# Rows 0 and 1 of the first feed-forward: 544 tokens at once in eight accumulators instead of 256 in four

## The chip, the cores and the metric

The kernel runs on one core of one Trainium2 chip. The core has TensorE (matrix products, PE in the profile; its weight loads are PEld), VectorE (DVE), ScalarE (ACT), GpSimd (POOL) and SyncE (SP, which here only issues loads and stores). Each engine takes its instructions in the order of its own queue and waits on the others by semaphores. Matmul results go to eight accumulators of 128 partitions x 512 float32 values, called banks here.

The metric is the time of one execution on the device in microseconds (us), as the median of several runs. A profile is one further execution, recorded by the hardware; its span runs from its first to its last instruction.

## The reference

One layer of a decoder trunk is computed for 512 prompt tokens and 8 x 4 sample tokens, 544 tokens in all, with 1024 features:

```python
def swiglu(x, wg, wu, wd):
    return (jax.nn.silu(x @ wg) * (x @ wu)) @ wd

x = layer_norm(ALPHA * x + 0.5 * swiglu(x, p["ffn1_wg"], p["ffn1_wu"], p["ffn1_wd"]), p["ln1_g"], p["ln1_b"])
...
x = layer_norm(ALPHA * x + mix, p["ln2_g"], p["ln2_b"])
x = layer_norm(ALPHA * x + 0.5 * swiglu(x, p["ffn2_wg"], p["ffn2_wu"], p["ffn2_wd"]), p["ln3_g"], p["ln3_b"])
```

`mix` comes from a time mixing (RWKV-7) and a short convolution side by side. `wg` and `wu` are 1024 x 2816 and `wd` is 2816 x 1024. The change lies in the first `swiglu`, at the very start of the program: in the first two of the 22 blocks of 128 hidden features, called rows here.

## The kernel before, in words

Tokens lie along the free dimension, features on the 128 partitions. x is kept transposed: eight blocks k of 128 features, each 128 x 544. The tokens are cut into two halves, `HALF = ((0, 256), (256, 544))`, of 256 and 288 tokens.

Every product is made of three matmuls. A number is split into a high part (ScalarE copies it to the rounded type, L134 and L138) and a low part (VectorE subtracts the high part, L135 and L139). The product is high x high, high x low and low x high. So a weight or an x block can be used by TensorE only when ScalarE has made its high part, and for two of the three matmuls VectorE must have followed.

A row m needs its gate (`g`) and its up (`u`) product: for each, eight blocks k of three matmuls, for each half of the tokens. ScalarE then takes the SiLU of the gate product out of its bank, and VectorE multiplies it by the up product.

The program starts as follows. GpSimd fills some constants; ScalarE loads the SiLU table at a first tiny activation (`warm`, L713) and makes the matrix `ones` (L716); four matmuls on constants run. Then SyncE issues the loads of the weights g0, u0, g1, u1 (called w0 to w3: rows 0 and 1) and of the first 256 tokens of x, in pieces of k: blocks 0 to 1, 2 to 3, then 4 to 7 (L722 to L741), each followed in the program by its split. After these, the other 288 tokens of x are loaded in four pieces (L744 and L745), then the two weights of row 2.

- `first_rows` (L431) multiplies the four weights with the 256 tokens, two k at a time across all four products, into four banks; then two SiLUs and two products.
- `main` (L666) goes on. For rows 0 and 1 it does the other 288 tokens (`up(m, 1)`), for rows 2 and 3 both halves. When a row is complete, `put_h` (L363) makes combinations of its two token halves, as needed by a Strassen-like scheme of later products, and splits them. Between the rows, one step of `inputs` (L449) makes and splits similar combinations of x (`next(tv)`).
- Then come the stages `downs` and `pairs` in turn (the scheme's products), whose weights are loaded and split ahead by a plan in units of TensorE work (`plan`, `feed`, `put`).

Banks come from two rings: `mm` (`big()`, three banks) and `sm` (`sm()`, five). `up` takes its banks from `mm`; `first_rows` had four from `sm`.

The order in each engine's queue is found by a scheduler that lists what is ready first. `tc.issue_after(ins)` puts the instructions of a block that run on the same engine as `ins` behind `ins` in its queue, without waiting for its end.

Of the kernel before, what the change touches and what calls it, by code (L numbers as in the profile page):

```python
# [12 lines left out]
F32 = mybir.dt.float32  # L13
F32R = mybir.dt.float32r
AF = mybir.ActivationFunctionType
OP = mybir.AluOpType
# [3 lines left out]
P = 128  # L20
D = 1024
KD = D // P
# [5 lines left out]
T = TP + NSEQ * TS  # L28
B11, B21, B22, NT1, NT2, T3, T4 = range(7)
HALF = ((0, 256), (256, 544))  # L30
# [31 lines left out]
def body(ctx: ExitStack, tc: tile.TileContext, xT, gu1, wd1, win, wo_c, wo_0, wo_1, gu2, wd2, lora, vec, cst,  # L62
         sst, cstate, s0, y_o, wkvp_o, wkvs_o, shift_o, conv_o):
    nc = tc.nc
    PE, ACT, DVE, POOL = nc.tensor, nc.scalar, nc.vector, nc.gpsimd
    dma = nc.sync.dma_start

    def pool(st, name, side="left", **kw):
        return st.enter_context(tc.tile_pool(name=name, bufs=1, side=side, reuse_waits="tile", **kw))
# [9 lines left out]
    xhl = keep.tile([P, 2, KD, T], F32R, name="xhl")  # L79
# [3 lines left out]
    cpb = keep.tile([P, 6 * TB], F32, name="cpb")  # L83
# [9 lines left out]
    def sm():  # L93
        return ps.tile([P, 512], F32, name="sm", bufs=5)
# [15 lines left out]
    def wtiles():  # L110
        return raw_tile(), hl_tile()

    def wload(src, n=1024, parts=1):
        raw, hl = wtiles()
        m = n // parts
        for i in range(parts):
            dma(raw[:, i * m:i * m + m], src[:, i * m:i * m + m])
            wsplit(hl, raw, i * m, i * m + m)
        return hl
# [12 lines left out]

    def wsplit(hl, raw, a, b):
        ACT.activation(hl[:, 0, a:b], raw[:, a:b], AF.Copy)  # L134
        DVE.tensor_tensor(hl[:, 1, a:b], raw[:, a:b], hl[:, 0, a:b].bitcast(F32), op=OP.subtract)  # L135

    def split(hi, lo, x):
        ACT.activation(hi, x, AF.Copy)  # L138
        DVE.tensor_tensor(lo, x, hi.bitcast(F32), op=OP.subtract)  # L139

    def block(hl, j, i):
        if isinstance(hl, tuple):
            hl, i = hl[i // 4], i % 4
        return hl[:, j, i * P:(i + 1) * P]
# [179 lines left out]
    class Ffn:  # L324
# [26 lines left out]
        def weights(self, key, src, n, pair=False):  # L351
            if key not in self.w:
                if pair:
                    raw, hl = raw_tile(), (self.hb_tile(), self.hb_tile())
                    dma(raw[:, 0:n], src)
                    for i in range(2):
                        wsplit(hl[i], raw[:, 512 * i:], 0, min(512, n - 512 * i))
                    self.w[key] = hl
                else:
                    self.w[key] = wload(src, n)  # L360
            return self.w[key]
# [68 lines left out]

        def first_rows(self, o):  # L431

            for a, b in ((0, 2), (2, 4), (4, 6), (6, 8)):
                for i in range(4):
                    hl = self.w["gu"[i % 2], i // 2]
                    for k in range(a, b):
                        for j, (v, y) in enumerate(((0, 0), (0, 1), (1, 0))):
                            PE.matmul(o[i][:, :256], block(hl, v, k), xhl[:, y, k, 0:256], start=(k == 0 and j == 0),
                                      stop=(k == KD - 1 and j == 2), skip_group_check=True)
            for m in range(2):  # L440
                s = self.rows[0][:, m, 0:256]
                ACT.activation(s, o[2 * m][:, :256], AF.Silu)
                DVE.tensor_tensor(s, s, o[2 * m + 1][:, :256], op=OP.mult)
            yield 0

        def first(self):
# [48 lines left out]
        def put(self, key, part):  # L495
# [5 lines left out]
            with ExitStack() as st:  # L501
                for e in self.held:
                    st.enter_context(tc.issue_after(e.ins))
                x = raws[key, "x"]
                if part == "b":
                    hi, lo = (hl[:, j].rearrange("p (q c) -> p q c", q=q) for j in range(2))
                    split(hi, lo, four(x)[:, :, 1])
                elif part == "a":
                    wsplit(hl, raws[key, "a"], 0, 1024)
                else:  # L510
                    if part == "y":
                        a, y = four(raws.pop((key, "a"))), four(raws.pop((key, "x")))
# [153 lines left out]
        def main(self):  # L666
            self.open_tv()
            tv = self.inputs()
            self.raw, self.held, self.t = {}, [], 0
            self.todo, self.events = self.plan()  # L670
            z = self.z
            self.done, self.made = set(), set()
            for i, m in enumerate((3, 0, 1, 2) if self.nf > NEX else range(self.na)):
                if m >= self.nf:
                    yield from self.up(m, 0)
                yield from self.up(m, 1)
                next(tv)
                if i == 1 and self.nf < self.na:
                    for j, n in enumerate("gu"):
                        self.w[n, 3] = wload(self.gu[3, :, j, :])  # L680
                elif i in (1, 2):
                    self.t = (-12, -5)[i - 1]
                    self.feed()
            self.t = 0
            for _ in tv:
                pass
            for d in range(KD):
                ACT.activation(z[:, d], z[:, d], AF.Copy, scale=2.0 * ALPHA)
            for ci in range(LAST + 1):
                if ci:  # L690
                    yield from self.pairs(ci)
                if ci < LAST:
                    yield from self.downs(ci)
            for d in range(KD):
                yield from self.down(LAST, d, 1 - self.late)
# [10 lines left out]
    z = pool(zst, "zp").tile([P, KD, T], F32, name="z")  # L706
# [3 lines left out]
    POOL.memset(one, 1.0)  # L710
    f1 = Ffn(z, gu1, wd1, "1", 2)
    f1.open()
    ACT.activation(warm, one, AF.Silu)  # L713
    POOL.memset(cpb[:, 0:256], 0.0)
    POOL.memset(cpb[:, 256:256 + P], 1.0 / D)
    ACT.activation(onr, cpb[:, 256:256 + P], AF.Copy)  # L716
    firsts = [sm() for _ in range(4)]
    for _ in range(4):
        PE.matmul(firsts[0][:, :256], cpb[:, 0:P], cpb[:, 0:256], start=True, stop=True)
    ws = [wtiles() for _ in range(4)]  # L720

    def first_w(i, a, b):  # L722
        raw, hl = ws[i]
        dma(raw[:, a * P:b * P], gu1[i // 2, :, i % 2, a * P:b * P])
        wsplit(hl, raw, a * P, b * P)

    def first_x(a, b, c0, c1):
        dma(z[:, a:b, c0:c1], xT[:, a:b, c0:c1])
        split(xhl[:, 0, a:b, c0:c1], xhl[:, 1, a:b, c0:c1], z[:, a:b, c0:c1])

    for a, b in ((0, 2), (2, 4), (4, 8)):
        first_w(0, a, b)
        for k in (a, a + 1) if a == 0 else ():
            first_x(k, k + 1, 0, 256)
        if a:
            first_x(a, a + 2, 0, 256)
        first_w(1, a, b)
        if b - a > 2:
            first_x(a + 2, b, 0, 256)
        first_w(2, a, b)  # L740
        first_w(3, a, b)  # L741
    for i, key in enumerate((("g", 0), ("u", 0), ("g", 1), ("u", 1))):
        f1.w[key] = ws[i][1]
    for k in range(0, KD, 2):  # L744
        first_x(k, k + 2, 256, T)  # L745
    for i, n in enumerate("gu"):
        f1.w[n, 2] = wload(gu1[2, :, i, :])
    dma(vc, vec)
# [12 lines left out]
    lo = cpb[:, 0:1024].rearrange("p (a t) -> p a t", a=2)  # L761
# [609 lines left out]
    z = pool(ctx, "zp2", "right").tile([P, KD, T], F32, name="z")  # L1371
# [194 lines left out]
```

## Time and profile before

| What | us |
|---|---|
| median of 3 runs | 1089.46 |
| shortest and longest run | 1087.12, 1090.7 |
| profiled execution | 1087.86 |
| its span | 1086.1 |
| TensorE busy in the span | 1057.3 |
| VectorE, ScalarE, GpSimd busy | 846.2, 588.7, 177.5 |

The granted TensorE clock was 0.998 of full speed. A busy TensorE counts each matmul from its start to its modelled end; matmuls overlap, so its pace is read from the distance of the starts. In the rows of the profile, a line number such as L438 is the line in the kernel; "out<-in" are the tiles written and read; `x96` is a count; "<-" names what ended the idle time before an instruction.

### The profile page before, as it was taken

The page shows a single profiled execution, that of the slowest core. Times are in us where ns is not written, and L with a number is a line of the kernel's source. Part 1 is how long each engine was busy: PE and PEld are TensorE (multiplying, and loading weights), DVE is VectorE, ACT ScalarE, POOL GpSimd, SP SyncE. Part 2 cuts the span into 40 slices and gives each one's busy share as a digit, 9 for nine tenths or more (in the row PEclk, how much of TensorE's full clock was granted, in tenths as well). Part 3 has the DMA queues.
Part 4 walks back from the last instruction along what each step waited for, and adds up shares of the span by engine and source line. Part 5 has one row for each costly group of instructions (what it writes and reads, how often), then busy time and mean ns, then how long its engine had stood idle before and what let it go on. Part 6 is the DMA issues. An engine that isn't in the chain of part 4 may idle for free.

```text
span 1086.1 us, 22868 instructions
## 1 busy us (share of the span) xinstructions
PE 1057.3 (97%) x9258; PEld 1018.5 (94%) x9258; DVE 846.2 (78%) x1576; ACT 588.7 (54%) x1095; POOL 177.5 (16%) x288
## 2 busy tenths in 40 slices
PE   9999999999999999999999999999999999999997
PEld 8999999999999988898889987999999999999996
DVE  7788888889675867775578558999889888888657
ACT  6655565555553677653445334667555565545425
POOL 0122220312200022141001200001312213121000
PEclk9999999999999999999999999999999999999999
DMA  8668595867854233243145625343857859677402
GB/s 280 138 124 191 121 217 132 177 156 148 187 117 154 80 114 84 59 111 85 42 141 185 146 78 178 117 136 78 184 152 153 196 119 211 154 156 177 122 1 83
DMA packets 99081, 148.88 MB, mean 137 GB/s; under 512 B 35232, under 2 KB 60576, under 8 KB 98976
## 3 DMA queue, kind: packets, MB, share of 16 engines
q1 hardware_dynamic: 71776, 111.25, 33.4%
q0 software_dynamic: 27200, 36.18, 22.0%
q8 instruction: 72, 1.18, 0.4%
q14 instruction: 33, 0.27, 0.1%
HBM read 128.74 MB, written 9.75 MB: 128 GB/s over the span
## 4 chain that ended last, share of the span: by engine, by line
PE 67%; issue 10%; DVE 9%; ACT 7%; DMA 6%; SPq 0%; POOL 0%; DVEq 0%; POOLq 0%; ACTq 0%
PE mm L150 7%; PE mm L547 7%; PE mm L151 7%; PE mm L548 7%; PE mm L549 7%; PE mm L152 7%; PE sm L549 5%; PE sm L548 5%; PE sm L547 5%; DMA raw<-in_gu 4%; ACT hl L134 3%; DVE hl L135 2%; PE sm L1047 1%; PE sm L150 1%; PE sm L151 1%
## 5 line engine op out<-in xcount | busy, mean ns | idle before, releaser
L135 DVE TENSOR_TENSOR hl<-raw,hl 128x1024 fp32r<-128x1024 f32 (+3 forms) x232 | 270.6, 1171 | 76.7 <-ACT hl L134 75.6
L134 ACT ACTIVATE hl<-raw 128x1024 fp32r<-128x1024 f32 (+3 forms) x232 | 232.0, 1013 | 90.4 <-DVE raw L514 40.9
L150 PE MATMUL mm<-xhl,hl 128*128 128x288 f32 (+1 forms) x736 | 218.8, 298 | 3.2 <-DVE z L1438 1.6
L151 PE MATMUL mm<-xhl,hl 128*128 128x288 f32 (+1 forms) x736 | 212.9, 289 | 0.3 <-DVE xhl L139 0.3
L152 PE MATMUL mm<-xhl,hl 128*128 128x288 f32 (+1 forms) x736 | 211.5, 288 | 0.1
L150 PEld LDWEIGHTS mm<-xhl,hl 128*128 128x128 f32 x736 | 138.0, 188 | 10.2 <-DVE z L1438 2.6
L151 PEld LDWEIGHTS mm<-xhl,hl 128*128 128x128 f32 x736 | 138.3, 188 | 2.5 <-issue 1.0
L152 PEld LDWEIGHTS mm<-xhl,hl 128*128 128x128 f32 x736 | 138.3, 188 | 1.1 <-DVE hl L135 0.5
L549 PE MATMUL sm<-xhl,hl 128*128 128x272 f32 x432 | 125.3, 290 | 0.0
L548 PE MATMUL sm<-xhl,hl 128*128 128x272 f32 x432 | 124.5, 288 | 0.0
L547 PE MATMUL sm<-xhl,hl 128*128 128x272 f32 x432 | 124.0, 287 | 0.0
L547 PE MATMUL mm<-tv,hl 128*128 128x272 f32 x288 | 83.3, 289 | 3.8 <-ACT cpb L608 2.0
L520 POOL DMA_DIRECT2D raw<-in_gu x36 | 43.4, 1206 | 258.1 <-DVE hlb L139 156.6
L549 PE MATMUL mm<-tv,hl 128*128 128x272 f32 x288 | 83.4, 290 | 0.0
L548 PE MATMUL mm<-tv,hl 128*128 128x272 f32 x288 | 83.1, 289 | 0.0
L547 PEld LDWEIGHTS sm<-xhl,hl 128*128 128x128 f32 x432 | 81.4, 188 | 0.0
L549 PEld LDWEIGHTS sm<-xhl,hl 128*128 128x128 f32 x432 | 81.3, 188 | 0.0
L548 PEld LDWEIGHTS sm<-xhl,hl 128*128 128x128 f32 x432 | 81.2, 188 | 0.0
L526 POOL DMA_DIRECT2D raw<-in_wd x32 | 39.3, 1481 | 249.1 <-DVE hlb L139 218.1
L547 PEld LDWEIGHTS mm<-tv,hl 128*128 128x128 f32 x288 | 54.3, 188 | 5.2 <-ACT cpb L608 3.1
L547 PE MATMUL mm<-hhl,hl 128*128 128x272 f32 x192 | 57.0, 302 | 0.7 <-DVE z L637 0.7
L547 PE MATMUL sm<-hhl,hl 128*128 128x272 f32 x192 | 55.9, 291 | 0.0
(393 smaller groups left out, 2785.5 us busy)
## 6 DMA issues: line engine op xcount, KB each, us to landing
raw<-in_gu SPq DMA_DIRECT2D x84, 512.0 KB, 4.6
raw<-in_gu POOLq DMA_DIRECT2D x36, 512.0 KB, 6.3
raw<-in_wd SPq DMA_DIRECT2D x32, 512.0 KB, 4.7
raw<-in_win SPq DMA_DIRECT2D x26, 512.0 KB, 3.7
raw<-in_wd POOLq DMA_DIRECT2D x32, 256.0 KB, 7.1
raw<-in_wd SPq DMA_DIRECT2D x16, 384.0 KB, 3.2
z<-cpb POOLq DMA_DIRECT2D x16, 272.0 KB, 9.4
z<-sv POOLq DMA_DIRECT2D x16, 272.0 KB, 6.5
```

Source lines behind the costliest of these rows:

```text
L134: ACT.activation(hl[:, 0, a:b], raw[:, a:b], AF.Copy)
L135: DVE.tensor_tensor(hl[:, 1, a:b], raw[:, a:b], hl[:, 0, a:b].bitcast(F32), op=OP.subtract)
L150: PE.matmul(out, wh, src[:, 0, k, c0:c1], start=(start and i == 0), stop=False)
L151: PE.matmul(out, wh, src[:, 1, k, c0:c1], start=False, stop=False)
L152: seen["fill"] = PE.matmul(out, wl, src[:, 0, k, c0:c1], start=False, stop=(stop and i == n - 1))
L520: POOL.dma_start(x.rearrange("p (s c) -> p s c", s=2), bass.AP(tensor=a11.tensor, offset=a11.offset, ap=[[2 * D, P], [P * 2 * D, 2], [1, 5 ...
L526: POOL.dma_start(four(x)[:, i], bass.AP(tensor=a11.tensor, offset=a11.offset, ap=[[DFF, P], [P * DFF, 2], [1, 256]]), accum_op=OP.add)
L547: PE.matmul(out, wh, src(0, i), start=(first and i == 0), stop=False, skip_group_check=True)
L548: PE.matmul(out, wh, src(1, i), start=False, stop=False, skip_group_check=True)
L549: PE.matmul(out, wl, src(0, i), start=False, stop=(i == n - 1), skip_group_check=True)
L1047: crit(PE.matmul(q[r0:r0 + m, o:o + nn], lhs, rhs, start=True, stop=True))
```

## The change

`first_rows` takes all 544 tokens. Each of its four products has two banks, one for each half, so all eight banks are in use: three of `mm` and five of `sm`. The order of the matmuls is by k and then by product for k = 0 to 5; for the last two k it is by product and then by k, so that g0 is done first and u1 last. Rows 0 and 1 need no `up` any more; `main` only calls `put_h` for them.

x is loaded whole, 544 tokens at a time. Its blocks 0 (in two halves) and 1 are loaded from ScalarE's queue, ahead of `warm`; the other six blocks in three loads from SyncE's. SyncE first issues the four weight pieces of k = 0 and 1. The matmuls' number and sizes are the same as before, only their order differs.

The combinations of x (`next(tv)`) are put behind the last weight split (`f1.head`) in VectorE's queue.

```diff
     def wsplit(hl, raw, a, b):
         ACT.activation(hl[:, 0, a:b], raw[:, a:b], AF.Copy)
-        DVE.tensor_tensor(hl[:, 1, a:b], raw[:, a:b], hl[:, 0, a:b].bitcast(F32), op=OP.subtract)
+        return DVE.tensor_tensor(hl[:, 1, a:b], raw[:, a:b], hl[:, 0, a:b].bitcast(F32), op=OP.subtract)
...
         def first_rows(self, o):
-            for a, b in ((0, 2), (2, 4), (4, 6), (6, 8)):
-                for i in range(4):
-                    hl = self.w["gu"[i % 2], i // 2]
-                    for k in range(a, b):
-                        for j, (v, y) in enumerate(((0, 0), (0, 1), (1, 0))):
-                            PE.matmul(o[i][:, :256], block(hl, v, k), xhl[:, y, k, 0:256], start=(k == 0 and j == 0),
-                                      stop=(k == KD - 1 and j == 2), skip_group_check=True)
+            order = [(k, i) for ks in ((0, 1), (2, 3), (4, 5)) for k in ks for i in range(4)]
+            order += [(k, i) for i in range(4) for k in (6, 7)]
+            for k, i in order:
+                hl = self.w["gu"[i % 2], i // 2]
+                for h, (c0, c1) in enumerate(HALF):
+                    for j, (v, y) in enumerate(((0, 0), (0, 1), (1, 0))):
+                        PE.matmul(o[i][h][:, :c1 - c0], block(hl, v, k), xhl[:, y, k, c0:c1], start=(k == 0 and j == 0),
+                                  stop=(k == KD - 1 and j == 2), skip_group_check=True)
             for m in range(2):
-                s = self.rows[0][:, m, 0:256]
-                ACT.activation(s, o[2 * m][:, :256], AF.Silu)
-                DVE.tensor_tensor(s, s, o[2 * m + 1][:, :256], op=OP.mult)
+                for h, (c0, c1) in enumerate(HALF):
+                    ACT.activation(self.rows[0][:, m, c0:c1], o[2 * m][h][:, :c1 - c0], AF.Silu)
+                for h, (c0, c1) in enumerate(HALF):
+                    s = self.rows[0][:, m, c0:c1]
+                    DVE.tensor_tensor(s, s, o[2 * m + 1][h][:, :c1 - c0], op=OP.mult)
             yield 0
...
         def main(self):
...
-                yield from self.up(m, 1)
-                next(tv)
+                if self.nf == 2 and m < 2:
+                    self.done.add(m)
+                    self.made.add(m)
+                    self.put_h(0, m, ("lo", "hi"))
+                    with tc.issue_after(self.head.ins):
+                        next(tv)
+                else:
+                    yield from self.up(m, 1)
+                    with ExitStack() as st:
+                        if self.nf == 2:
+                            st.enter_context(tc.issue_after(self.head.ins))
+                        next(tv)
...
+    def load_x(eng, a, b, c0, c1):
+        eng.dma_start(z[:, a:b, c0:c1], xT[:, a:b, c0:c1])
+
+    def split_x(a, b, c0, c1):
+        split(xhl[:, 0, a:b, c0:c1], xhl[:, 1, a:b, c0:c1], z[:, a:b, c0:c1])
+
+    for h in range(2):
+        load_x(ACT, 0, 1, *HALF[h])
+    load_x(ACT, 1, 2, 0, T)
     ACT.activation(warm, one, AF.Silu)
...
-    firsts = [sm() for _ in range(4)]
+    firsts = [f() for f in (big, big, big, sm, sm, sm, sm, sm)]
+    firsts = [firsts[2 * i:2 * i + 2] for i in range(4)]
...
-    for a, b in ((0, 2), (2, 4), (4, 8)):
-        first_w(0, a, b)
-        for k in (a, a + 1) if a == 0 else ():
-            first_x(k, k + 1, 0, 256)
-        if a:
-            first_x(a, a + 2, 0, 256)
-        first_w(1, a, b)
-        if b - a > 2:
-            first_x(a + 2, b, 0, 256)
-        first_w(2, a, b)
-        first_w(3, a, b)
+    def load_w(i, a, b):
+        dma(ws[i][0][:, a * P:b * P], gu1[i // 2, :, i % 2, a * P:b * P])
+
+    def split_w(i, a, b):
+        return wsplit(ws[i][1], ws[i][0], a * P, b * P)
+
+    for i in range(4):
+        load_w(i, 0, 2)
+        split_w(i, 0, 2)
+        if i == 0:
+            for h in range(2):
+                split_x(0, 1, *HALF[h])
+        elif i == 1:
+            split_x(1, 2, 0, T)
+    for a, b in ((2, 4), (4, 8)):
+        load_x(nc.sync, a, a + 2, 0, T)
+        split_x(a, a + 2, 0, T)
+        for i in range(4):
+            load_w(i, a, b)
+            f1.head = split_w(i, a, b)
+        if b - a > 2:
+            load_x(nc.sync, a + 2, b, 0, T)
+            split_x(a + 2, b, 0, T)
...
-    for k in range(0, KD, 2):
-        first_x(k, k + 2, 256, T)
```

More of the change, by code (lines that the diff above doesn't have):

```diff
@@ L716, in body @@
     ACT.activation(onr, cpb[:, 256:256 + P], AF.Copy)
-    firsts = [sm() for _ in range(4)]
+    firsts = [f() for f in (big, big, big, sm, sm, sm, sm, sm)]
+    firsts = [firsts[2 * i:2 * i + 2] for i in range(4)]
     for _ in range(4):
-        PE.matmul(firsts[0][:, :256], cpb[:, 0:P], cpb[:, 0:256], start=True, stop=True)
+        PE.matmul(firsts[0][0][:, :256], cpb[:, 0:P], cpb[:, 0:256], start=True, stop=True)
     ws = [wtiles() for _ in range(4)]
[L722 to L729, printed above, removed]
-    for a, b in ((0, 2), (2, 4), (4, 8)):
-        first_w(0, a, b)
-        for k in (a, a + 1) if a == 0 else ():
-            first_x(k, k + 1, 0, 256)
-        if a:
-            first_x(a, a + 2, 0, 256)
-        first_w(1, a, b)
+    def load_w(i, a, b):
[16 more added lines that the diff above has]
+            f1.head = split_w(i, a, b)
         if b - a > 2:
-            first_x(a + 2, b, 0, 256)
-        first_w(2, a, b)
-        first_w(3, a, b)
+            load_x(nc.sync, a + 2, b, 0, T)
+            split_x(a + 2, b, 0, T)
     for i, key in enumerate((("g", 0), ("u", 0), ("g", 1), ("u", 1))):
         f1.w[key] = ws[i][1]
-    for k in range(0, KD, 2):
-        first_x(k, k + 2, 256, T)
     for i, n in enumerate("gu"):
```

## The prediction

> **What bounds the kernel now.** I read the totals first. TensorE is busy for 97% of the span and leads the chain that ended last, so a change pays only where TensorE stands still.
>
> ```profile
> PE 1057.3 (97%) x9258; PEld 1018.5 (94%) x9258; DVE 846.2 (78%) x1576; ACT 588.7 (54%) x1095; POOL 177.5 (16%) x288
> ...
> PE 67%; issue 10%; DVE 9%; ACT 7%; DMA 6%; SPq 0%; POOL 0%; DVEq 0%; POOLq 0%; ACTq 0%
> ```
>
> Next, TensorE's timeline around the changed stage (start, length, what).
>
> ```profile
> 4.46 1.84 PE L438 MATMUL sm<-xhl,hl 128*128 128x256 f32 x6
> ...
> 12.93 0.38 PE L438 MATMUL sm<-xhl,hl 128*128 128x256 f32 x1 [0.76 <-ACT xhl L138]
> 13.66 5.79 PE L438 MATMUL sm<-xhl,hl 128*128 128x256 f32 x47 [0.34 <-DVE xhl L139]
> 19.29 0.29 PE L150 MATMUL mm<-xhl,hl 128*128 128x288 f32 x1
> ...
> 31.98 0.28 PE L150 MATMUL mm<-xhl,hl 128*128 128x256 f32 x1
> ```
>
> The 96 matmuls of rows 0 and 1 over 256 tokens (L438) run from 4.46 to 19.29; the 96 over the other 288 tokens follow until row 2 starts at 31.98. The pace is the distance of starts: (19.29 - 13.66) / 47 = 0.120 us for 256 columns, (31.98 - 19.29) / 96 = 0.132 us for 288. At these paces the two parts need 11.5 + 12.7 = 24.2 us, and they took 31.98 - 4.46 = 27.5 us. **The 3.3 us between are all that this stage can give back**; they lie before 13.66, where 49 matmuls (5.9 us) took 9.2 us.
>
> Why TensorE is held there: ScalarE waits for loads, and behind it VectorE and TensorE wait for the split halves.
>
> ```profile
> 0.75 1.28 ACT L713 ACT_TABLE_LOAD   x1 [0.75 <-PEq L1546]
> 2.04 0.20 ACT L713 ACTIVATE warm<-eps 128x1 f32<-128x1 f32 x1
> 2.15 0.29 ACT L716 ACTIVATE ones<-cpb 128x128 fp32r<-128x128 f32 x1
> 3.46 0.42 ACT L134 ACTIVATE hl<-raw 128x256 fp32r<-128x256 f32 x1 [1.02 <-DMA raw<-in_gu]
> 3.79 0.40 ACT L138 ACTIVATE xhl<-z 128x256 fp32r<-128x256 f32 x1
> ...
> 10.50 0.42 ACT L134 ACTIVATE hl<-raw 128x256 fp32r<-128x256 f32 x1 [1.35 <-DMA raw<-in_gu]
> ```
>
> The same start by windows (from:to, length, then busy time and instructions of TensorE, its weight loads, VectorE, ScalarE and GpSimd, clock, share of the DMA engines, GB/s) shows what the loads deliver, and that VectorE has room from row 2 on.
>
> ```profile
> 2.00:5.00 3.00, 3.00 (x9) 2.37 (x8) 0.82 (x3) 1.66 (x7) 0.00 (x0) 1.00 0.83 256
> 5.00:8.00 3.00, 3.00 (x21) 3.00 (x20) 1.98 (x5) 1.60 (x5) 0.00 (x0) 1.00 0.83 245
> 8.00:11.00 3.00, 2.97 (x23) 2.58 (x22) 1.41 (x4) 1.57 (x4) 0.00 (x0) 1.00 0.71 192
> 11.00:14.00 3.00, 1.89 (x14) 1.50 (x13) 2.15 (x4) 2.23 (x4) 0.00 (x0) 1.00 1.06 389
> ...
> 31.90:55.90 24.00, 24.00 (x195) 24.00 (x195) 15.82 (x29) 13.74 (x26) 5.02 (x4) 1.00 0.55 111
> ```
>
> **The change part by part.** Loads are issued by SyncE in order, and each of the first takes 0.40 to 0.45 us of its queue (0.89 / 2):
>
> ```profile
> 0.75 0.40 SPq L724 DMA_DIRECT2D raw<-in_gu  x1
> 1.21 0.89 SPq L728 DMA_DIRECT2D z<-in_xT  x2
> ```
>
> *Matmuls.* None is added or removed: 192 stay, 24.2 us. What changes is how much of each arriving pair of k-blocks feeds TensorE: 24 x 0.120 = 2.9 us before, 24 x (0.120 + 0.132) = 6.05 us after. One (k, row) step is 0.755 us.
>
> *ScalarE's three issues.* No row shows a load issued from ScalarE. Bounds: nothing, or what GpSimd takes, 1206 ns (row below). SyncE's 0.43 us is the nearest row, since like the loads moved it is a plain load without arithmetic; I take it. The three stand ahead of the table load: ScalarE, which finished `ones` 1.69 us after 0.75, is free at 0.75 + 1.29 + 1.69 = 3.73 instead of 2.44. The cover is the 1.02 us that it waited for the first weights, so the first split moves from 3.46 to 3.73. With free issues it stays at 3.46; at GpSimd's price it is 6.06.
>
> ```profile
> L520 POOL DMA_DIRECT2D raw<-in_gu x36 | 43.4, 1206 | 258.1 <-DVE hlb L139 156.6
> ```
>
> The Trainium skill ("DMA: Bandwidth & Descriptors", section "Issuing engines are not separate DMA queues") says that all issuers share the same DMA engines and their transfers interleave, so that a second issuer saves issue time alone. By it the first weights (128 KB) would share the engines with the first 128 KB of x and land up to 0.5 us later (128 KB at the 256 GB/s of 2 to 5 us), at 3.97 instead of 3.46, and the sum below would be worse by 0.2 us. No row before shows two queues at work in this stage.
>
> *The ramp.* Splits, by these rows and by the distance of starts above (0.33 us on ScalarE for 256 columns; x pieces from the 544- to 576-column forms):
>
> ```profile
> L138 ACT ACTIVATE xhl<-z 128x576 fp32r<-128x576 f32 x4 | 2.5, 676 | 0.0
> ...
> L135 DVE TENSOR_TENSOR hl<-raw,hl 128x1024 fp32r<-128x1024 f32 x4 | 4.9, 1218 | 0.0
> L135 DVE TENSOR_TENSOR hl<-raw,hl 128x256 fp32r<-128x256 f32 x8 | 3.2, 423 | 5.7 <-ACT hl L134 5.6
> L139 DVE TENSOR_TENSOR xhl<-z,xhl 128x576 fp32r<-128x576 f32 x4 | 2.9, 753 | 0.3 <-ACT xhl L138 0.3
> ```
>
> ScalarE makes the high halves of w0, x0 (two pieces), w1, x1, w2, w3 from 3.73 to 6.40; VectorE's low halves end at 4.61, 4.95, 5.33, 5.66, 6.49, 6.85 and 7.20. TensorE starts at 4.5, waits about 0.5 us for x0's first low half, 0.1 us for its second and 0.3 us for w2's, and ends k = 0 at 8.15 and k = 1 at 8.15 + 4 x 0.755 = 11.17. Without any wait from 4.46 it would be 10.5.
>
> *Later pairs.* k = 2 and 3 need 2.16 MB (1.05 of weights, 1.11 of x). At the 231 GB/s that 2 to 11 us average, 2.1 MB are in at 11.0, and then 389 GB/s are delivered: complete about 11.3. Add 0.85 us for the two splits of the last quarter: 12.2, against 11.17 + 3 x 0.755 = 13.4 when row u1 first needs it. Block 4 to 8 needs 2.2 MB more, 6 us at 389 GB/s, so 17.3 at the latest for all of it; TensorE reaches k = 4 at 17.2, where only x and w0 are needed. I add 0.2 us for a hiccup here (ends: 0, and 1.5 us if the 192 GB/s of 8 to 11 us lasted on: 2.16 MB after 11.2 us, in at 13.2).
>
> *End of the stage.* 11.17 + 24 x 0.755 + 0.2 = 29.5 for row 2's first matmul, against 31.98: **2.5 us gained.**
>
> *Eight banks.* Row 2 takes the first `mm` bank again. Its gate g0 is done three rows of two k before the end (6 x 0.755 = 4.5 us), at 25.0, and a SiLU of about 0.4 us (next row group) frees it: 25.4 against 29.5. The later two banks are freed by 26.9. Cost nothing, cover 4 us.
>
> *SiLUs, products, `put_h`.* The same instructions, now bunched at 25 to 33 us:
>
> ```profile
> L442 ACT ACTIVATE hk<-sm 128x256 f32<-128x256 f32 x2 | 0.8, 385 | 1.0 <-PE sm L438 1.0
> ...
> L458 DVE TENSOR_TENSOR cpb<-z 128x544 f32<-128x544 f32 x2 | 1.4, 719 | 0.0
> ...
> L443 DVE TENSOR_TENSOR hk<-hk,sm 128x256 f32<-128x256 f32 x2 | 0.8, 414 | 0.0
> ```
>
> VectorE must have the row-2 weights (two splits of 1.22 us) ready by 29.5; what stands before them is 3.4 us (eight weight splits at 0.42), 2.8 us (four of 512 columns, by the line between 0.42 and 1.22 at 0.69) and about 5.5 us of x, with their own 2.4 us 14 us of work from 4 us on: about 11 us of room. The transforms in `inputs` (about 0.72 us each) are only queued behind the last weight split; they are first needed in `pairs`, behind rows 2 and 3 and the first `downs`. The stage from 31.9 to 55.9 moves 2.5 us earlier against a VectorE that is free for 8.2 of 24 us there.
>
> *SyncE.* 15 loads instead of 21 stand before row 2's weights, so these start sooner. GpSimd's queue is not passed. What is late next is TensorE's own work.
>
> The profiled execution took 1087.86 us, 1.8 us more than its span, so the sum is 1085.4. The median shown, 1089.46, is 1.6 us above it; I carry the 2.5 us over and predict 1087.0.
>
> **Rivals.**
> 1. *The start is late or the loads are short:* ScalarE's issues cost GpSimd's price (first split 6.06, 2.3 us lost) or the 1.5 us hiccup happens. Gain 0.2 to 1.2 us, about 1088.7. For it: the 192 GB/s window. Against: SyncE's 0.43 us, and a supply that need only be half as dense per matmul.
> 2. *A queue turns it round (slower):* on VectorE, an in-order engine, the row-2 splits stand behind products and `put_h` of rows 0 and 1, which now wait for the last matmul at 29.5. Two products (0.86 with the larger half), six `put_h` steps of about that size (2.6) and the split (1.22) stop TensorE for 4.7 us: 2.2 us slower, 1091.7; with five transforms of 0.72 between, 5.8 us slower, 1095. It decides once that stall passes 2.5 us. Against: the row-2 weights arrive some 10 us earlier than the products' inputs.
> 3. *Everything goes and something follows:* free issues, no ramp wait, the whole 3.3 us, and a later stage's order improves a little: 1086.0 or lower. Against: TensorE cannot start before x is split.
> 4. *The 2.5 us are given back in the `downs` and `pairs` stages* because weights come late: 1089.5. Against: TensorE's two longest waits in these stages (the waits over the whole span: in total, times, longest) are for ScalarE's copies of its own results; no load and no weight split.
>
> ```profile
> PE mm L547 <- ACT cpb L608: 2.0, 4, 1.0
> ...
> PE mm L547 <- ACT cpb L614: 1.8, 1, 1.8
> ```
>
> **How the numbers follow.** A measurement of this kernel can tell about 0.3%, 3.3 us, from no change. Forecast (1.5 to 3.2 us gained) 0.50; rival 1 0.15; rival 2 0.15; rival 3 0.13; rival 4 0.07. Low end: the shortest run, 1087.12, less 3.3 and 0.8 for a better later order, 1083.0. High end: rival 2's first price and a little, 1092.0. Faster by over 0.3%: rival 3 and a part of the forecast that lies near the bound, 0.23. Slower by over 0.3%: most of rival 2, 0.12. Between them 0.65. By itself the forecast spans 1086.2 to 1088.0.
>
> **What would show it.** The first L438-type matmul at 4.5 to 4.8; no wait of TensorE over 0.5 us after 8 us; row 2's first matmul (128x256) near 29.5; then every stage 2.5 us earlier, the end included. The three issues on ScalarE's queue should take 0.4 us each. I am wrong if row 2 waits for VectorE, if the first split comes after 4.5, or if the shift of row 2 is not the shift of the kernel's end.

## The result and the profile after

Over 20 executions of each kernel on the same chip the changed kernel took 1086.86 us (median; 1082.39 to 1091.17) and the kernel before 1089.95 us (1086.36 to 1094.53). The ratio is 0.9969, with a 95% interval of 0.9955 to 0.9984: faster, by 3.1 us between the medians and by 1.7 to 4.9 us with the interval. The profiled execution took 1082.39 us (span 1080.6), the shortest of its 20, so its end is no fair picture of the median; its start lies among those of the repeats below.

The totals and the chain that ended last, of the changed kernel: TensorE still leads, with 1.2 us less busy time and 5.5 us less span.

```profile
span 1080.6 us, 22860 instructions
...
PE 1056.1 (98%) x9258; PEld 1017.5 (94%) x9258; DVE 845.5 (78%) x1573; ACT 587.1 (54%) x1092; POOL 177.3 (16%) x288
...
PE 75%; DVE 8%; ACT 7%; issue 6%; DMA 4%; POOL 0%; ACTq 0%; DVEq 0%; POOLq 0%
```

TensorE's timeline of the changed stage (start, length, what). The 192 matmuls of rows 0 and 1 are now all on L439, and row 2 begins at 30.48 instead of 31.98.

```profile
4.76 0.58 PE L439 MATMUL mm<-xhl,hl 128*128 128x256 f32 x1
5.59 1.73 PE L439 MATMUL mm<-xhl,hl 128*128 128x288 f32 x8 [0.25 <-ACT xhl L138]
7.16 2.54 PE L439 MATMUL sm<-xhl,hl 128*128 128x288 f32 x15
9.54 1.27 PE L439 MATMUL mm<-xhl,hl 128*128 128x256 f32 x9
...
12.54 1.25 PE L439 MATMUL mm<-xhl,hl 128*128 128x256 f32 x9
...
27.11 3.53 PE L439 MATMUL sm<-xhl,hl 128*128 128x288 f32 x27
30.48 0.28 PE L150 MATMUL mm<-xhl,hl 128*128 128x256 f32 x1
```

The rows split the stage in two. k = 0 (24 matmuls) lasts from 4.76 to 9.54, 4.78 us. From there each k takes 3.00 us (9.54 to 12.54), and the 168 matmuls up to 30.48 take 20.94 us, 0.125 us each, without a wait. The whole loss is in k = 0, which at that pace would have taken 3.0 us.

ScalarE's timeline of the same start: the three loads on its queue, then what it waits for.

```profile
0.74 1.39 ACTq L728 DMA_DIRECT2D z<-in_xT  x3
2.16 1.28 ACT L736 ACT_TABLE_LOAD   x1 [2.16 <-issue]
...
3.99 0.42 ACT L134 ACTIVATE hl<-raw 128x256 fp32r<-128x256 f32 x1
4.31 0.40 ACT L138 ACTIVATE xhl<-z 128x256 fp32r<-128x256 f32 x1
5.10 0.44 ACT L138 ACTIVATE xhl<-z 128x288 fp32r<-128x288 f32 x1 [0.39 <-DMA z<-in_xT]
5.45 0.40 ACT L134 ACTIVATE hl<-raw 128x256 fp32r<-128x256 f32 x1
6.75 0.66 ACT L138 ACTIVATE xhl<-z 128x544 fp32r<-128x544 f32 x1 [0.91 <-DMA z<-in_xT]
7.32 0.71 ACT L134 ACTIVATE hl<-raw 128x256 fp32r<-128x256 f32 x2
```

Block 1 of x (x1) arrives last (6.75), and the splits of w2 and w3, which k = 0 needs, stand behind it in ScalarE's queue (7.32). The same start by windows (columns as in the prediction): 8 to 11 us held 23 matmuls before and holds 24 now, but 11 to 14 us held 14 and holds 26; the DMA engines deliver 332 instead of 192 GB/s in 8 to 11.

```profile
5.00:8.00 3.00, 2.70 (x15) 2.17 (x15) 1.55 (x4) 2.00 (x5) 0.00 (x0) 1.00 1.03 362
8.00:11.00 3.00, 3.00 (x24) 2.88 (x24) 2.22 (x5) 2.37 (x6) 0.00 (x0) 1.00 0.98 332
11.00:14.00 3.00, 3.00 (x26) 3.00 (x25) 2.46 (x5) 2.33 (x4) 0.00 (x0) 1.00 0.97 361
```

The start of the matmuls hides something that the busy column doesn't show. Distances between the starts of the matmuls, in us, listed from the traces:

```
before  4.46 0.57 (5.04), then 0.21 eight times up to 6.75, 0.19, then 0.12 from 6.93 on
after   4.76 0.83 0.41 0.21 0.21 0.21 (6.64) 0.16, then 0.11 to 0.13 from 6.80 on, but for
        0.35 0.22 (ends at 7.77, 7.99) and 0.18 0.22 (ends at 8.56, 8.79)
```

Up to 6.93 and 6.80 us the two kernels run at 0.213 us per 256 columns, about half the later pace, while the granted clock in the windows reads 1.00. That 1.00 is no measurement: the clock's first record in these two traces begins at 6.89 and 6.68, just where the full pace begins, and a window without a record prints 1.00. In the other traces of the kernels that follow, the first record begins anywhere from 5.10 to 7.30 us (without the order: 13.77), so the time at half pace differs from execution to execution.

### The profile page after: what moved, and what is told of

Read it like the earlier page. It is cut to its first block, busy times and chain, and to the rows that moved or that the text cites. A ratio compares the mean times of both kernels' runs of the same rounds, so it can differ in the third digit from the quotient of the medians.

```text
span 1080.6 us, 22860 instructions
## 1 busy us (share of the span) xinstructions
PE 1056.1 (98%) x9258; PEld 1017.5 (94%) x9258; DVE 845.5 (78%) x1573; ACT 587.1 (54%) x1092; POOL 177.3 (16%) x288
## 4 chain that ended last, share of the span: by engine, by line
PE 75%; DVE 8%; ACT 7%; issue 6%; DMA 4%; POOL 0%; ACTq 0%; DVEq 0%; POOLq 0%
PE mm L550 9%; PE mm L551 8%; PE mm L552 8%; PE mm L150 7%; PE mm L151 6%; PE mm L152 6%; PE sm L552 6%; PE sm L550 6%; PE sm L551 6%; DMA raw<-in_gu 3%; ACT hl L134 2%; PE sm L439 1%; PE sm L1072 1%; DVE hl L135 1%; PE sm L150 1%
## 5 line engine op out<-in xcount | busy, mean ns | idle before, releaser
L150 PE MATMUL mm<-xhl,hl 128*128 128x288 f32 (+1 forms) x704 | 209.5, 298 | 3.2 <-DVE z L1463 1.6
L151 PE MATMUL mm<-xhl,hl 128*128 128x288 f32 (+1 forms) x704 | 203.5, 289 | 0.3 <-DVE xhl L139 0.3
L152 PE MATMUL mm<-xhl,hl 128*128 128x288 f32 (+1 forms) x704 | 202.1, 287 | 0.1
L150 PEld LDWEIGHTS mm<-xhl,hl 128*128 128x128 f32 x704 | 132.1, 188 | 10.1 <-DVE z L1463 2.6
L151 PEld LDWEIGHTS mm<-xhl,hl 128*128 128x128 f32 x704 | 132.4, 188 | 2.5 <-issue 1.0
L152 PEld LDWEIGHTS mm<-xhl,hl 128*128 128x128 f32 x704 | 132.3, 188 | 1.1 <-DVE hl L135 0.5
L550 PE MATMUL mm<-hhl,hl 128*128 128x272 f32 x192 | 57.0, 302 | 0.6 <-DVE z L640 0.6
L551 PE MATMUL mm<-hhl,hl 128*128 128x272 f32 x192 | 55.8, 290 | 0.0
```

Source lines behind the costliest of these rows:

```text
L150: PE.matmul(out, wh, src[:, 0, k, c0:c1], start=(start and i == 0), stop=False)
L151: PE.matmul(out, wh, src[:, 1, k, c0:c1], start=False, stop=False)
L152: seen["fill"] = PE.matmul(out, wl, src[:, 0, k, c0:c1], start=False, stop=(stop and i == n - 1))
L550: PE.matmul(out, wh, src(0, i), start=(first and i == 0), stop=False, skip_group_check=True)
L551: PE.matmul(out, wh, src(1, i), start=False, stop=False, skip_group_check=True)
```

## The experiments

The theory: the gain is made at the start of the stage, between the first matmul and row 2, and is only passed on behind it; k = 0 limits it, by data (ScalarE's order and the loads), and perhaps by the half pace. The rivals: the start time of TensorE, ScalarE's load queue, or a stage behind row 2 makes the difference. The table collects all runs; the first three columns come from the traces. "To the end" is from row 2's first matmul to the start of the last matmul. Each ratio is to executions of the kernel before on the same chip.

| Kernel | first matmul of rows 0, 1 | row 2's first | to the end | median us (executions) | ratio to before, 95% |
|---|---|---|---|---|---|
| before | 4.46 | 31.98 | 1046.6 | 1089.95 (20) | |
| before, again | 4.46 | 31.71 | 1045.4 | 1086.42 (1) | |
| after | 4.76 | 30.48 | 1042.5 | 1086.86 (20) | 0.9969 (0.9955 to 0.9984) |
| after, again | 4.80 | 30.94 | 1045.4 | 1090.38 (12) | 0.9992 (0.9974 to 1.0010) |
| x by SyncE | 4.46 | 30.60 | 1046.6 | 1090.75 (12) | 0.9994 (0.9968 to 1.0019) |
| x1 behind w3 | 4.78 | 30.12 | 1051.6 | 1089.53 (12) | 0.9985 (0.9962 to 1.0008) |
| late start | 6.58 | 30.85 | 1050.1 | 1088.24 (12) | 0.9978 (0.9962 to 0.9994) |
| without the order | 5.08 | 34.20 | 1048.2 | 1091.91 (1) | |
| before with x by ScalarE | 4.74 | 31.03 | 1050.3 | 1090.66 (1) | |
| g0 last | 4.79 | 34.98 | 1050.3 | 1094.69 (1) | |
| last chunk held in rows | 4.76 | 30.27 | 1044.5 | 1088.01 (12) | 0.9983 (0.9961 to 1.0005) |
| x1 behind w3, and held in rows | 4.66 | 29.96 | 1050.5 | 1087.93 (12) | 0.9990 (0.9972 to 1.0007) |

**The same two kernels again.** No edit; the point is how much of the first pair's difference comes back.

> The changed kernel once more, unchanged. Theory A (the stage gives 1.5 us for good, and what the profiled executions differ beyond that is the waits of ScalarE for GpSimd's accumulating stores and late weights, which change from one execution to the next): row 2's first matmul again at 30.5 us, within 0.2; the gaps of TensorE ahead of the first product of tv in `pairs` differ from those of the other execution by up to 2 us; median 1.5 to 3.5 us under the kernel before. Theory B (the earlier start moves the later transfers apart for good): those gaps stay at 0.2 to 0.6 us as in the other execution, and the median is 4 us or more under the kernel before.

> The kernel before once more, unchanged, for a second profile. Theory A (from one execution to the next the late waits vary, the start does not): row 2's first matmul at 32.0 us, within 0.3; the time from there to the last matmul, 1046.6 us in the first profile of it, is anywhere from 1042 to 1052, as in the five profiles with the change (1042.5 to 1051.6). Theory B (the change also shortens what follows): it stays above 1046.

Row 2 came at 30.94 in the one, outside the 0.2 us that I allowed, and 31.71 in the other, and the median was 0.6 us under the kernel before instead of 1.5 to 3.5. Before, the two traces have 31.98 and 31.71 (mean 31.85); after, they have 30.48 and 30.94, and a later kernel with the same start 30.27 (mean 30.56). The change of the stage is 1.3 us, of marks that themselves differ by 0.3 and 0.7 us. In the second pair of profiles it is passed on unchanged: 0.8 us at row 2 (31.71 against 30.94) and the same 1045.4 us from there to the end. But the end differs from execution to execution of one kernel: from row 2 on, the changed kernel took 1042.5 and 1045.4 us. One wait that varies this way is ScalarE's for a transfer of `sv` (timelines near 285 us, in this order: before, before again, after, after again):

```profile
286.60 0.43 ACT L572 ACTIVATE sv<-cpb 128x272 f32<-128x272 f32 x1 [3.80 <-DMA z<-sv]
```

```profile
285.20 0.43 ACT L572 ACTIVATE sv<-cpb 128x272 f32<-128x272 f32 x1 [2.23 <-DMA z<-sv]
```

```profile
282.36 0.43 ACT L575 ACTIVATE sv<-cpb 128x272 f32<-128x272 f32 x1 [2.04 <-DMA z<-sv]
```

```profile
284.17 0.43 ACT L575 ACTIVATE sv<-cpb 128x272 f32<-128x272 f32 x1 [2.34 <-DMA z<-sv]
```

The kernel before waited 3.80 us in one execution and 2.23 in the next. TensorE's wait behind such copies goes the same way (waits of before again: in total, times, longest; those of before stand in the prediction):

```profile
PE mm L547 <- ACT cpb L608: 1.2, 3, 0.5
PE mm L547 <- ACT cpb L614: 0.2, 1, 0.2
```

The 1.8 us on which the prediction's rival 4 was judged was 0.2 us in another execution of the same program. So of the 5.65 us by which the first profile of the changed kernel ends its matmuls sooner (1072.95 against 1078.60), 1.5 lie ahead of row 2 and 1.75 between 280 and 300 us, where this wait stands; the other 2.4 arose at several places and were not traced to a wait.

What goes with the column "to the end" is TensorE's clock. In six traces the clock's records show full speed from row 2 to the last matmul (before, before again, after, after again, x by SyncE, last chunk held in rows), and they took 1042.5 to 1046.6 us. The other six have one to three stretches of 3.41 us at half the clock, and took 1048.2 to 1051.6 us. What follows: this change is to be judged at row 2's first matmul.

**x from SyncE's queue, behind w0 and w1.** This undoes the part with ScalarE's queue alone.

```diff
-    for h in range(2):
-        load_x(ACT, 0, 1, *HALF[h])
-    load_x(ACT, 1, 2, 0, T)
...
             for h in range(2):
+                load_x(nc.sync, 0, 1, *HALF[h])
                 split_x(0, 1, *HALF[h])
         elif i == 1:
+            load_x(nc.sync, 1, 2, 0, T)
             split_x(1, 2, 0, T)
```

> Undoes one part: x's blocks 0 and 1 are loaded from SyncE's queue, behind w0 and w1. If a second issuer saves issue time alone and the transfers share the engines (theory A), ScalarE's first split goes back to about 3.5, x1 lands near 6 to 6.5, the other weights some 0.5 us later, and row 2 starts at 30.2 to 30.7, the time within 0.5 us of the changed kernel. If ScalarE's queue brings x in beside the weights at the engines' spare rate (rival), row 2 starts at 31.2 or later.

Row 2 came at 30.60, inside the 30.27 to 30.94 of the change as it is. ScalarE, from this kernel's timeline:

```profile
3.46 0.42 ACT L134 ACTIVATE hl<-raw 128x256 fp32r<-128x256 f32 x1 [1.02 <-DMA raw<-in_gu]
...
8.32 0.42 ACT L134 ACTIVATE hl<-raw 128x256 fp32r<-128x256 f32 x1 [0.94 <-DMA raw<-in_gu]
```

The first weights come at 3.46 again instead of 3.99, and the fourth weight split runs at 8.32 where in the changed kernel it had ended by 8.03 (two from 7.32 in 0.71). What the second queue brings forward at one place it takes at another; in this one trace ScalarE's queue is worth nothing measurable in the changed kernel.

**x by ScalarE's queue in the kernel before.** The reverse: that part alone.

```diff
+    for k in range(2): ACT.dma_start(z[:, k:k + 1, 0:256], xT[:, k:k + 1, 0:256])
     ACT.activation(warm, one, AF.Silu)
...
-        for k in (a, a + 1) if a == 0 else ():
-            first_x(k, k + 1, 0, 256)
+        for k in (a, a + 1) if a == 0 else (): split(xhl[:, 0, k:k + 1, 0:256], xhl[:, 1, k:k + 1, 0:256], z[:, k:k + 1, 0:256])
```

> One part alone, on the kernel before: the 256 tokens of x's blocks 0 and 1 are loaded from ScalarE's queue ahead of its table load, nothing else. With x_sync this makes the square of the two parts. If a second issuer saves issue time alone: ScalarE's first split moves from 3.46 to about 4.0, the later loads come two issues (0.9 us) sooner, and row 2 starts at 31.4 to 32.0, against 31.7 and 32.0 in the two profiles of the kernel before. If ScalarE's queue carries the gain, row 2 starts at 31.0 or earlier.

Row 2 came at 31.03, 0.8 us sooner than the mean before: more than I expected, in one execution. Its windows and ScalarE's timeline say why:

```profile
8.00:11.00 3.00, 3.00 (x28) 3.00 (x27) 1.30 (x4) 1.18 (x4) 0.00 (x0) 1.00 0.92 299
11.00:14.00 3.00, 2.10 (x16) 1.70 (x15) 2.67 (x5) 2.74 (x5) 0.00 (x0) 1.00 1.07 387
```

```profile
3.96 0.42 ACT L134 ACTIVATE hl<-raw 128x256 fp32r<-128x256 f32 x1 [0.59 <-DMA raw<-in_gu]
```

In 8 to 11 us 299 GB/s arrive instead of 192, and 28 matmuls run instead of 23. The first weights come later, at 3.96, and ScalarE waits 0.59 us for them, as it would if the two queues share the engines. So the second queue seems to help the old order, where loads limit, and not the new one. As far as one trace of each can show, the two parts of the change are not additive: 0.8 us for the queue alone, 1.25 us (31.85 to 30.60) for the 544 tokens with their order alone, 1.3 us for both.

**Block 1 of x split behind w3.**

```diff
-        elif i == 1:
+        elif i == 3:
             split_x(1, 2, 0, T)
```

> One move in the program: x1 is split behind w2 and w3 instead of ahead of them. In the changed kernel ScalarE stood 0.9 us for x1 with w2 and w3 behind it in its queue. If that order is what the start lacked against the forecast, TensorE's gaps at 7.4 to 8.8 us go (0.35 + 0.1 + 0.1), k = 0 ends near 9.0 and row 2 starts at 29.9 to 30.1. If w2 and w3 have not landed by then either, row 2 stays at 30.4.

ScalarE no longer waits for x1 ahead of w2 and w3 (this kernel's timeline; they are split from 6.18 instead of 7.32):

```profile
6.18 0.81 ACT L134 ACTIVATE hl<-raw 128x256 fp32r<-128x256 f32 x2 [0.63 <-DMA raw<-in_gu]
6.90 0.64 ACT L138 ACTIVATE xhl<-z 128x544 fp32r<-128x544 f32 x1
```

k = 0 ends at 9.18 instead of 9.54 and row 2 comes at 30.12, 0.4 us sooner than the mean; in the second trace with this edit (last row of the table) they are at 9.03 and 29.96. The in-order queue of ScalarE was a part of the loss. At the end nothing of it is left in the profiled execution, and the ratio, 0.9985, can't be told from the others.

**The start held back.** Eight matmuls on constants instead of four keep TensorE from the rows' matmuls for 1.8 us more.

```diff
-    for _ in range(4):
+    for _ in range(8):
         PE.matmul(firsts[0][0][:, :256], cpb[:, 0:P], cpb[:, 0:256], start=True, stop=True)
```

> Eight matmuls on constants instead of four ahead of the first useful one; TensorE then starts near 7.4 to 8.2 and nothing it needs is late. If the losses of the start are waits for data and the slow pace of the first matmuls alone, the 192 matmuls take 24.0 us without a gap, and row 2 starts at 31.4 to 32.2. Theory A: the time follows, 0.9 to 1.7 us over the changed kernel and at most 0.6 us under the kernel before by this stage alone. Rival (the place of later work against the transfers decides, not the start): the time does not follow the start of row 2.

```profile
6.58 1.46 PE L439 MATMUL mm<-xhl,hl 128*128 128x256 f32 x9
...
9.91 1.26 PE L439 MATMUL mm<-xhl,hl 128*128 128x256 f32 x9
```

These rows are TensorE's timeline. The first matmul comes at 6.58, sooner than the 7.4 to 8.2 that I expected and 1.8 us later than in the changed kernel, but k = 0 ends at 9.91 and row 2 comes at 30.85. Both lie inside the range of the traces that start at 4.8 (9.32 to 10.01 and 30.27 to 30.94), and row 2 comes sooner than the 31.4 to 32.2 that I expected. The changed kernel loses those 1.8 us again in waits for splits. When TensorE starts is not what binds. That this kernel has the second-best ratio of all, 0.9978, says how little the medians rank these versions.

**Without the order behind the last weight split.** Both uses of `issue_after` are taken out, so the transforms of `inputs` stand in VectorE's queue where the scheduler puts them.

```diff
-                    with tc.issue_after(self.head.ins):
-                        next(tv)
+                    next(tv)
...
-                    with ExitStack() as st:
-                        if self.nf == 2:
-                            st.enter_context(tc.issue_after(self.head.ins))
-                        next(tv)
+                    next(tv)
```

> Undoes one part: the combinations of x are no longer put behind the last weight split in VectorE's queue. One of them then stands first in that queue and needs x's blocks 0 and 1, which land at 6.7 us; the first weight's low half, made from 4.4 us in the changed kernel, waits behind it. This is the forecast's rival of a queue that turns the change round: row 2 starts 2 to 3 us later than 30.5 to 30.9, at 32.5 to 34, later than in the kernel before. If VectorE's queue has room at the start, row 2 stays under 31.3.

VectorE's first instructions, and TensorE's timeline, of this kernel:

```profile
6.45 0.73 DVE L461 TENSOR_TENSOR cpb<-z 128x544 f32<-128x544 f32 x1 [6.45 <-DMA z<-in_xT]
7.10 0.42 DVE L135 TENSOR_TENSOR hl<-raw,hl 128x256 fp32r<-128x256 f32 x1
```

```profile
5.08 1.22 PE L439 MATMUL mm<-xhl,hl 128*128 128x256 f32 x3
7.90 1.49 PE L439 MATMUL mm<-xhl,hl 128*128 128x256 f32 x5 [1.60 <-DVE xhl L139]
```

A transform (L461) is first in VectorE's queue and waits for x1; the first weight's low half is made at 7.10. In the changed kernel it is at 4.44 (its VectorE timeline):

```profile
4.44 0.42 DVE L135 TENSOR_TENSOR hl<-raw,hl 128x256 fp32r<-128x256 f32 x1 [4.44 <-ACT hl L134]
```

TensorE stops for 1.60 us, from 6.30 to 7.90; then, from 8.28, the distance of starts stays 0.21 to 0.24 us until 13.72. Row 2 comes at 34.20, 3.6 us behind the change as it is and 2.4 us behind the kernel before. Most of this is pace and not the wait itself: the 25 distances from 7.90 to 13.72 took 5.82 us and would take about 3.1 at 0.125, which is up to 2.7 of the 3.6 us. So the change is faster only with this order; without it, VectorE's queue makes the stage slower, which is what rival 2 said of another place in that queue.

**g0 last.** The last two k take the products in reverse, so that the bank that row 2 needs is finished last and the cover of the eight banks is gone.

```diff
-            order += [(k, i) for i in range(4) for k in (6, 7)]
+            order += [(k, i) for i in (3, 2, 1, 0) for k in (6, 7)]
```

> The changed kernel with the last two k in the reverse order of products, so that g0, whose bank row 2 takes first, ends last and not first. The forecast put the banks at no cost with 4 us of cover. Without the cover TensorE must wait at row 2's first matmul for g0's last matmul (0.3 us to its end), ScalarE's SiLU (0.39 us) and the signals: a gap of 0.5 to 0.9 us there, where the changed kernel has 0.13. If the gap stays at 0.13, the cover was not needed.

TensorE and then ScalarE, timelines of this kernel:

```profile
29.35 1.65 PE L439 MATMUL mm<-xhl,hl 128*128 128x256 f32 x12
34.98 0.39 PE L150 MATMUL mm<-xhl,hl 128*128 128x256 f32 x1 [3.98 <-ACT hk L443]
```

```profile
31.79 1.06 ACT L134 ACTIVATE hl<-raw 128x1024 fp32r<-128x1024 f32 x1
32.73 0.66 ACT L701 ACTIVATE z<-z 128x544 f32<-128x544 f32 x1
33.28 0.43 ACT L138 ACTIVATE hhl<-hk 128x272 fp32r<-128x272 f32 x1
33.60 1.05 ACT L134 ACTIVATE hl<-raw 128x1024 fp32r<-128x1024 f32 x1
34.55 0.68 ACT L443 ACTIVATE hk<-mm 128x256 f32<-128x256 f32 x2
```

The last matmul of g0 ends at 31.0; its SiLU, which frees the bank, starts at 34.55, since g1's two SiLUs (31.23 to 31.90) and the four instructions of the first four rows stand ahead of it in ScalarE's queue. I had priced the lost cover at the SiLU alone; TensorE stood still for 3.98 us, because the queue ahead of it came on top. The banks are free only by the order of the last two k.

**The last chunk held in `rows`.** This is no test of the change: the `sv` wait above stands in every trace with `sv`, and here the intermediate of the last chunk is held in `rows[0]` instead, with nothing left out.

```diff
-                s = self.rows[0] if ci < LAST and j == 0 else sv
+                s = self.rows[0] if j == 0 else sv
```

> The changed kernel with one more move, far from the start: in the last `pairs` of each feed-forward the first pair of rows is made in the tile hk instead of sv, whose rows GpSimd's accumulating stores still read when ScalarE reaches it. If ScalarE's wait for those stores (2.0 to 3.9 us at 283 to 291 us, with TensorE's gaps of 0.3 to 2.1 us behind it) is the largest part of what varies after row 2, the two gaps ahead of the first product of tv there go to 0.2 us in every execution and the median falls 1 to 2 us under the changed kernel's. If the weights' loads are what is late, the gaps stay.

> Both moves together: x1 split behind w2 and w3, and hk in the last `pairs`. Row 2 at 30.1 as with the first alone; the gap at 287 us and that at 983 us at 0.2 us; 2.5 to 4 us under the kernel before.

The second kernel has this edit and x1 behind w3. The wait on `sv` is gone in both traces. The medians are 1088.01 and 1087.93 us beside 1088.94 us of the kernel before (ratios 0.9983 and 0.9990). The expected 1 to 2 us under the changed kernel and 2.5 to 4 us under the kernel before did not show, and neither can be told from the changed kernel. The second has the earliest row 2 of all (29.96), and lost it again, in part where TensorE's clock was lower; windows of it and of the changed kernel:

```profile
300.00:400.00 100.00, 98.05 (x755) 96.77 (x755) 71.18 (x124) 52.67 (x95) 7.17 (x31) 0.98 0.38 110
```

```profile
300.00:400.00 100.00, 98.06 (x766) 96.75 (x765) 72.07 (x124) 54.00 (x96) 8.97 (x35) 1.00 0.37 109
```

At a granted clock of 0.98 instead of 1.00, TensorE started 755 instead of 766 matmuls in these 100 us: 1.4 us at 0.13 us each. This is one of its three half-clock stretches (at 391.9, 426.0 and 566.0 us).

## Why the prediction was right or wrong

**The time.** 1087.0 was forecast and 1086.86 came, inside the range; by the ratio the gain is 0.31%, right at the bound of 0.3% between faster and no difference, where the forecast had put it just short of that. That it came so close is luck: the stage gave 1.3 us, not 2.5. The first comparison allows 1.7 to 4.9 us for the whole kernel, the second -1.1 to 2.8 us. In the second, the mean granted clock of every execution is known (12 of the changed kernel, 35 of the one before), and the time falls by about 1.3 us for each 0.001 that the clock is higher. At an equal clock the changed kernel is there 1.75 us shorter (0.9 to 2.6 at 95%, an estimate by a straight line of time over clock, with one slope for both groups). The stage's 1.3 us fit this without a further gain behind row 2; what the first comparison shows beyond that stays open, since the clocks of its executions of the kernel before are not on record.

**"The 3.3 us between are all that this stage can give back"** was a bound, but too wide. In the profile of the kernel before, eight distances from 5.04 to 6.75 were 0.213 instead of 0.120 us and the ninth 0.19: 0.8 us (8 x 0.093 + 0.07) were pace, not waiting, and feeding TensorE more work cannot return them. In that execution at most 2.5 us were to be had, just what the forecast took with nothing lost; in one whose full pace begins sooner it is up to 0.8 us more.

**ScalarE's three issues** took 1.39 us, 0.46 each, for the 0.43 taken from SyncE: right. The first split came at 3.99 instead of 3.73. ScalarE was done with `ones` at 3.85 (3.56 + 0.29), 0.12 later than forecast; the old kernel with two such issues waited 0.59 us and split at 3.96, so the weights themselves came later with two queues at work. The Trainium skill ("DMA: Bandwidth & Descriptors", section "Issuing engines are not separate DMA queues") said that they interleave. By it the prediction had 3.97 in a sentence beside the sum, and the traces agree (3.96, 3.99); I should have let it into the range of this step.

**The ramp** is the step that failed. k = 0 was to end at 8.15 and ended at 9.54, 1.39 us later. 0.27 us of this is a slip of my own: 4.5, the waits of 0.9 and 4 x 0.755 add to 8.42. The other 1.12 us are the landing of x1, for which the sum has no term. It lets ScalarE split x1 as soon as its queue comes to it, at about 5.1 (3.73 and four splits of 0.33 to 0.35); x1 came at 6.75, and w2 and w3 waited behind it. ScalarE's row for x1 in the three other traces with this start (after again, last chunk held in rows, g0 last), and TensorE's first matmul on w2 in after again:

```profile
7.22 0.66 ACT L138 ACTIVATE xhl<-z 128x544 fp32r<-128x544 f32 x1 [1.47 <-DMA z<-in_xT]
```

```profile
6.53 0.66 ACT L138 ACTIVATE xhl<-z 128x544 fp32r<-128x544 f32 x1 [1.18 <-DMA z<-in_xT]
```

```profile
7.11 0.66 ACT L138 ACTIVATE xhl<-z 128x544 fp32r<-128x544 f32 x1 [1.49 <-DMA z<-in_xT]
```

```profile
8.24 1.93 PE L439 MATMUL sm<-xhl,hl 128*128 128x256 f32 x12 [1.09 <-ACT hl L134]
```

k = 0 ended at 9.54 in after, and at 10.01, 9.32 and 9.90 in these three: 2.79 us behind the start of x1's split each time. Neither the half pace nor the later start (4.76) adds to it. In after again the full pace was there by 5.74, sooner than in after, and TensorE only waited longer for w2; with the start held back to 6.58, k = 0 ended at 9.91. Why x1 lands so late stays open; loaded by SyncE it was split at 6.41. With x1 split behind w3 the loads of w2 and w3 and the pace are next, and k = 0 ends at 9.18 and 9.03.

**Later pairs.** The 0.2 us hiccup did not come: from 9.54 on each k took 3.00 us, against 3.02 forecast. From the end of k = 0 to row 2 it took 20.94 us instead of 21.35, which gave 0.41 us back: 1.39 - 0.41 = 1.0 us, row 2 at 30.48 instead of 29.5.

**Eight banks** cost nothing, as said, but the cover was 3.2 us, not 4: the SiLUs of g0 ran from 26.63 on and were done by 27.29 (ScalarE's timeline of the changed kernel).

```profile
26.63 0.66 ACT L443 ACTIVATE hk<-mm 128x256 f32<-128x256 f32 x2
```

Why it costs nothing was argued too simply, as the run with g0 last shows: the SiLU must also find ScalarE's queue free.

**VectorE and SyncE.** Right: the two splits of the row-2 weights stood ahead of the products, and the second was done at 22.63, 7.9 us ahead of need.

```profile
19.53 1.22 DVE L135 TENSOR_TENSOR hl<-raw,hl 128x1024 fp32r<-128x1024 f32 x1
...
21.41 1.22 DVE L135 TENSOR_TENSOR hl<-raw,hl 128x1024 fp32r<-128x1024 f32 x1
```

That the transforms "are only queued behind the last weight split" was named as harmless; it is more than that: without it row 2 came 3.6 us later.

**The rivals.** 1 (late start, short loads): neither of its two causes came, since the issues cost 0.46 us and the later loads kept up; a load that was short is what failed, but at x1, which it did not name. Its size did half come: 1.3 us lies between its 0.2 to 1.2 and the forecast's 1.5 to 3.2. 2 (slower by a queue): not in this kernel; both kernels that spoil a queue's order, on VectorE and on ScalarE, are slower than before up to row 2, by 2.4 and 3.1 us. 3 (everything goes): the start of TensorE was later, not earlier, and row 2 came nowhere near 28.7, so its reason fails, although the first profile, at 1082.39 us, looks like it. 4 (given back behind row 2): no load or weight split took the gain; but the distance to the end varies by 9 us between the traces here (1042.5 to 1051.6), so 1 us given back could not be seen in one trace; in the second pair of profiles none was.

## What to carry to other kernels

Read the pace of the matmuls in a start-up stage before calling its missing time idle: a part of it may be pace, and a later wait may cover that part again. On an in-order engine, a split that waits for a late load holds all behind it, and the same goes for the instruction that frees a bank: look at what the queue has ahead of it, not at its own length. When a program differs from itself by several us from one execution to the next, judge a change of 1 us by a mark close behind it, in two or more traces, and not by the end.

## What the runs showed of the hardware

Matmuls ran at half pace at two kinds of places. At the start, the kernels before and after had 0.21 us for 256 columns until their clock's first record, at 6.89 and 6.68 us; ahead of it the profile's granted clock reads 1.00 for want of a record. After a stop of 3.98 us (g0 last) the first matmuls ran at 0.12, then for 3.4 us at 0.21, and there the row of the windows shows it, a granted clock of 0.50:

```profile
35.00:36.00 1.00, 1.00 (x8) 1.00 (x9) 1.00 (x2) 1.00 (x3) 0.00 (x0) 1.00 0.76 123
36.00:39.40 3.40, 3.40 (x18) 3.40 (x17) 3.40 (x8) 2.42 (x4) 0.00 (x0) 0.50 0.83 246
39.40:42.80 3.40, 3.40 (x31) 3.40 (x30) 2.27 (x5) 1.86 (x4) 0.00 (x0) 1.00 0.14 57
```

18 matmuls in 3.40 us against 31 in the next 3.40: a stop of 4 us costs about 1.6 us more behind it. The Trainium skill ("TensorE: Matmul & The Clock Gate", section "What's actually happening") says that the array runs at half clock until it has been busy for a window of about 3.4 us, and falls back after an idle window; the 3.4 us here agree with it. That a whole idle window is needed does not agree: the nine other half-clock stretches of these traces, 3.41 us each, came within 4 us of stops of 0.97 to 1.96 us, the longest there. And a stop does not settle it: one of 1.9 us between 420 and 432 us stands in all twelve traces, and the clock halved behind it in two. A stop of 1.60 us ahead of the first full pace (the kernel without the order) put the full pace off to 13.72, 5.8 us after the matmuls went on. That is longer than one such window; its clock record begins at 13.77, so the 3.41 us ahead of it, from 10.4, lie wholly behind the stop, while the 3.41 us before those still hold its end (6.9 to 10.4).
